# Output projection: eight of 32 row blocks of six chunks in seven products of 2x2 blocks instead of eight

## Chip, cores and metric

The kernel runs on one core of a Trainium2 chip. The metric is the device time of one execution in microseconds (us). The time before is the median of three runs. Engines are named as in the profile: PE is TensorE's matrix multiply and PEld its weight load, DVE is VectorE, ACT is ScalarE, POOL is GpSimd, SP is SyncE, which here only issues transfers (DMAs).

## What is computed

One encoder block on 256 tokens of width 4096, all in float32. Attention and Fourier mixing each give a branch; the branches are gated and merged, projected once more, added to the input and normalised:

```python
def reference(x, norm_gain, w_in, gate_bias, w_branch_attn, w_branch_fourier, w_out, final_norm_gain):
    ...
        h = rms_norm(x, norm_gain[layer])
        proj = h @ w_in[layer]
        ...
        branch_attn = (o_attn * jax.nn.silu(z_attn)) @ w_branch_attn[layer]
        ...
        branch_four = (y_four * jax.nn.silu(z_four)) @ w_branch_fourier[layer]
        ...
        mixed = jax.nn.sigmoid(g_attn) * branch_attn + jax.nn.sigmoid(g_four) * branch_four
        x = x + mixed @ w_out[layer]
    return rms_norm(x, final_norm_gain)
```

The change is in the last two lines: `mixed @ w_out` is a product of 256x4096 by 4096x4096.

## The kernel before

**Matrix products.** The 256 tokens are two halves of 128 (`t` = 0, 1). The weights of a product are read in chunks of 512 columns (`CW`) and, within a chunk, in row blocks of 128 (`k`); `w_out` has 8 chunks of 32 row blocks. Each float32 operand is split into a high half, rounded to the PE's format (`F32R`), and a low half, the rest. A product of two blocks is three matmuls into the same accumulator: high by high, high by low, low by high. The tokens' halves `m_hi` and `m_lo` are kept in SBUF; the weights are split as they come. Each matmul has a 128x128 block of tokens as the loaded operand and 128x512 of weights as the moving one.

**One chunk** is one call of `gemm` (line 236). Its `load` issues a DMA of four row blocks (1 MB) into one of three buffers `wt`, then takes a pair of row blocks at a time: ACT writes the high half (`wh`, 128x1024) and DVE subtracts it from the weights to make the low half (`wl`). `run(i)` issues the split of step i+1, then pending small tasks (`step`), then the twelve matmuls of step i (two row blocks, two halves of tokens, three matmuls). So a chunk is 16 steps.

**Buffers.** `turn` hands out the `wh` and `wl` buffers in rotation: three of each, and more when `spare` lists free tiles (line 231). A buffer is written again only when PE has finished the step that used it, so the number of buffers limits how far ACT and DVE can be ahead of PE. In the output projection there are three sets up to chunk 5 and seven from chunk 6 on.

**Tasks.** Other DVE and ACT work is put in between the splits: a task is a generator that yields the cost of its next piece and a delay in steps, and `step` runs pieces while a budget of 1.45 us a step lasts. `add` (line 881) adds a finished chunk to the residual `x` (in `res`), takes the sum of squares on ACT, and multiplies by the gain `fg`; it begins four steps after the chunk's end. All engines work strictly in the order in which the program issues their instructions.

**The end.** Chunk 7 runs with `LAG` 5: the second half of the tokens goes five steps behind the first, so that the first half's normalisation and stores lie beside matmuls. `last` (line 897) adds, normalises and stores a half.

Of the kernel before, what the change touches and what calls it, by code (L numbers as in the profile page):

```python
# [10 lines left out]
F32 = mybir.dt.float32  # L11
F32R = mybir.dt.float32r
AF = mybir.ActivationFunctionType
ALU = mybir.AluOpType
# [3 lines left out]
P = 128  # L18
D = 4096
SEQ = 256  # L20
NT = SEQ // P
KT = D // P
CW = 512
# [9 lines left out]
WG = 4  # L33
WS = 2
LAG = 5
# [2 lines left out]
BUDGET_U = 0.75  # L38
CAP = 2.7
LEAD = 3  # L40

Q0, K0, V0, ZA0, U0, ZF0, G0 = 0, 3072, 6144, 9216, 10240, 12288, 14336

# [50 lines left out]
def hybrid_block(ctx: ExitStack, tc: tile.TileContext, x, norm_gain, w_in, gate_bias, w_attn,  # L94
                 w_four, w_out, final_gain, rope, mask, dft, out):
    nc = tc.nc
    x = x[0]
    w_in, w_attn, w_four, w_out = w_in[0], w_attn[0], w_four[0], w_out[0]
    pe, dve, act, sp = (InOrder(tc, e) for e in (nc.tensor, nc.vector, nc.scalar, nc.sync))
# [16 lines left out]
    def lower(i, shape, dtype, name):  # L116

        return low.tile(shape, dtype, tag=f"low{i}", name=name)
# [17 lines left out]
    def spawn(task, urgent=True, after=()):  # L136

        t = Task(task, urgent, clock.now + (2 if pending else 0), after)
        if urgent:
            tasks.insert(sum(u.urgent for u in tasks), t)  # L140
        else:
            tasks.append(t)
        return t
# [6 lines left out]
    def finish(these):  # L150
        flush()
        complete(these)

    def complete(these):
        for t in list(these):
            complete(t.after)
            while t in tasks:
                if not t.run(clock.now):
                    tasks.remove(t)
# [17 lines left out]
    def rows(a, t, s):  # L177

        return a.rearrange("(m q) d -> q m d", q=2)[t, :, s]
# [47 lines left out]
    def turn(name, shape, dtype):  # L227
        n = turns[name] = turns.get(name, -1) + 1
        if name == "wt":
            return wtp.tile(shape, dtype, name=f"wt{n % 3}")  # L230
        n %= 3 + len(spare)
        if n < 3:
            return wpool.tile(shape, dtype, name=f"{name}{n}")
        return lower(2 * spare[n - 3] + (name == "wl"), shape, dtype, f"{name}{n}")

    def gemm(accs, hi, lo, w, c0, lag=0, during=None, loading=None, at=None, between=None):

        nk = w.shape[0] // P  # L240
        wv = w[:, c0:c0 + CW].rearrange("(k p) n -> p k n", p=P)
        wt = None
        steps = []

        def load(k):
            nonlocal wt
            if k >= nk:
                return
            single = loading is not None and k == 0
            if k % WG == 0:  # L250
                wt = turn("wt", [P, WG, CW], F32)
                pieces = [(0, WG)] if not single else [(0, 1), (1, 2), (2, WG)]
                for a, b in pieces:
                    sp.dma_start(wt[:, a:b, :], wv[:, k + a:k + b, :])
                    if loading is not None:
                        loading(k + b)
            wh = turn("wh", [P, WS, CW], F32R)
            wl = turn("wl", [P, WS, CW], F32R)
            for j in range(0, WS, 1 if single else WS):
                n = slice(j, j + (1 if single else WS))  # L260
                split(wt[:, k % WG + n.start:k % WG + n.stop, :], wh[:, n], wl[:, n])
            steps.append((wh, wl))

        def multiply(i, j, t):
            if not 0 <= i < len(steps):
                return
            wh, wl = steps[i]
            k = i * WS + j
            a, b = hi[:, k, t * P:(t + 1) * P], lo[:, k, t * P:(t + 1) * P]
            pe.matmul(accs[t], a, wh[:, j, :], start=(k == 0), stop=False)  # L270
            pe.matmul(accs[t], a, wl[:, j, :], start=False, stop=False)
            pe.matmul(accs[t], b, wh[:, j, :], start=False, stop=(k == nk - 1))

        def run(i):
            load((i + 1) * WS)
            if during is not None:
                during(i * WS)
            if at is not None and i == at[0]:
                at[1]()
            step()  # L280
            for j in range(WS):
                for t in range(NT):
                    multiply(i - lag * t, j, t)
                if between is not None and j == 0:
                    between(i * WS)

        load(0)
        flush()
        if during is not None:
            during(-WS)  # L290
        last = nk // WS + lag - 1
        for i in range(last):
            run(i)
        pending.append(lambda: run(last))
# [3 lines left out]
    def new_accs():  # L298
        n = turns["acc"] = turns.get("acc", -1) + 1
        complete(users[n % 2])  # L300
        return [ps_mm.tile([P, CW], F32, name=f"acc{n % 2}{t}") for t in range(NT)]

    def use(task, after=()):

        users[turns["acc"] % 2] = [spawn(task, after=after)]
        return users[turns["acc"] % 2]
# [376 lines left out]
    def mixed():  # L683
        nonlocal sz
        finish(mixing)
        fo.close()
        sz = pool(ctx, "szp").tile([P, NT, 2 * CW], F32, name="sz")
        users[1 - slot] = [spawn(silu_za(0))]
# [185 lines left out]
    with ExitStack() as st:  # L874
        op = pool(st, "op")
        RW = 2 * CW
        res = [[op.tile([P, RW], F32, name=f"res{t}{i}") for i in range(D // RW)] for t in range(NT)]
        parts = op.tile([P, NT, 8], F32, name="fparts")
        fgs = [op.tile([P, CW], F32, name=f"fg{c % 2}") for c in range(8)]

        def add(c, accs):
            s = slice(c * CW, (c + 1) * CW)
            sp.dma_start(fgs[c], final_gain[None, s].to_broadcast([P, CW]))
            if c % 2 == 0:
                for t in range(NT):
                    sp.dma_start(res[t][c // 2], rows(x, t, slice(c * CW, c * CW + RW)))
            yield 0.0, 0
            for t in range(NT):
                rt = res[t][c // 2][:, c % 2 * CW:(c % 2 + 1) * CW]
                yield 0.75, 4 if t == 0 else 0  # L890
                dve.tensor_add(rt, rt, accs[t])
                junk = op.tile([P, CW], F32, name="junk2")
                act.activation(junk, rt, AF.Square, accum_out=parts[:, t, c:c + 1])
                yield 0.6, 0
                dve.tensor_mul(rt, rt, fgs[c])

        def last(accs, t):
            rt = res[t][3][:, CW:]
            yield 0.7, 0
            dve.tensor_add(rt, rt, accs[t])  # L900
            junk = op.tile([P, CW], F32, name="junk2")
            act.activation(junk, rt, AF.Square, accum_out=parts[:, t, 7:8])
            yield 1.0, 0
            ssq = small.tile([P, 1], F32, name="ssq")
            dve.tensor_add(ssq, parts[:, t, 7:8], sums[t])
            r = small.tile([P, 1], F32, name="rstd_o")
            rstd_of(r, ssq)
            for n, (c0, c1) in enumerate(((0, 256), (256, 1024), (1024, 2048), (2048, 3072), (3072, 3584), (3584, 4096))):
                o = res[t][c0 // RW][:, c0 % RW:(c1 - 1) % RW + 1]
                if c0 == 7 * CW:  # L910
                    dve.scalar_tensor_tensor(o, o, r, fgs[7], op0=ALU.mult, op1=ALU.mult)
                elif n % 2:
                    act.activation(o, o, AF.Copy, scale=r)
                else:
                    dve.tensor_scalar(o, o, r, None, op0=ALU.mult)
                sp.dma_start(rows(out[0], t, slice(c0, c1)), o)

        sums = [op.tile([P, 1], F32, name=f"sum{t}") for t in range(NT)]

        def summed():  # L920
            yield 0.2, 2
            for t in range(NT):
                dve.reduce_sum(sums[t], parts[:, t, 0:7], axis=AX.X)

        use(add(0, first))
        for c in range(1, 7):
            accs = new_accs()
            if c == 6:
                spare.extend(range(4))
            gemm(accs, m_hi, m_lo, w_out, c * CW)  # L930
            added = use(add(c, accs))
        spawn(summed(), after=added)
        accs = new_accs()
        sp.dma_start(fgs[7], final_gain[None, 7 * CW:].to_broadcast([P, CW]))
        gemm(accs, m_hi, m_lo, w_out, 7 * CW, LAG, at=(KT // WS, lambda: finish([spawn(last(accs, 0))])))
        finish(list(tasks))
        finish([spawn(last(accs, 1))])

# [50 lines left out]
```

## Time and profile before

| | |
|---|---|
| Median of 3 runs | 2536.12 us (2535.91 to 2537.52) |
| Profiled execution | 2535.88 us |
| Its span | 2534.1 us |
| Granted PE clock, mean over the span | 0.998 |
| Bytes moved by DMA | 529.60 MB, 209 GB/s on average |

A row of a group of instructions reads: line, engine, operation, output <- inputs, shapes, count, then total busy time and mean duration in ns of one, then the idle time ahead of them and what ended it. A row of the timeline reads: start, duration (us), engine, line, operation, and in brackets the idle time ahead and its releaser. A matmul's record lasts longer than its slot, because matmuls overlap in the array.

### The profile page before, as it was taken

To read this page: it belongs to the slowest core of one execution; us is meant where nothing else is said; L and a number is where in the kernel's file an instruction comes from. 1 tells how busy PE (TensorE), PEld (TensorE's weight loads), DVE (VectorE), ACT (ScalarE), POOL (GpSimd) and SP (SyncE) were. 2 spreads that over 40 slices of the span, in tenths; PEclk is the share of its full clock that TensorE was granted. 3 is DMA by queue.
4 is the path that set the end of the run, shared out by engine and by line. 5 is a ranking of instruction groups with operands and counts; after the bars stand their busy time and mean duration, and the time that the engine had idled before them with its cause. 6 is when DMAs were issued, how large, how long until landed. Compare 5 with 4: busy or idle time off the path is not lost.

```text
span 2534.1 us, 29976 instructions
## 1 busy us (share of the span) xinstructions
PE 2518.7 (99%) x11646; PEld 2102.9 (83%) x11646; DVE 1768.8 (70%) x2546; ACT 1121.3 (44%) x1340; POOL 77.7 (3%) x146
## 2 busy tenths in 40 slices
PE   9999999999999999999999999999999999999998
PEld 7888888888888888888888888888888888888886
DVE  6778887777753575848689584878656888754554
ACT  5544544454443434343443434344544444444443
POOL 0000000000000000000000000000100000000000
PEclk9999999999999999999999999999999999999999
DMA  7677666666655565555555555555766665656674
GB/s 256 239 251 233 233 234 227 236 232 217 221 177 172 190 196 187 198 195 188 187 175 190 193 198 189 194 187 179 253 232 216 225 230 188 218 189 223 218 245 150
DMA packets 252846, 529.60 MB, mean 209 GB/s; under 512 B 9984, under 2 KB 10784, under 8 KB 252704
## 3 DMA queue, kind: packets, MB, share of 16 engines
q1 hardware_dynamic: 237056, 471.89, 56.2%
q0 software_dynamic: 15600, 55.78, 6.5%
q8 instruction: 91, 1.49, 0.3%
q14 instruction: 51, 0.42, 0.0%
q10 hardware_dynamic: 48, 0.02, 0.0%
HBM read 512.97 MB, written 14.68 MB: 208 GB/s over the span
## 4 chain that ended last, share of the span: by engine, by line
PE 97%; DMA 1%; DVE 1%; issue 0%; ACT 0%; SPq 0%; DVEq 0%; ACTq 0%
PE acc L53 91%; PE pt L53 3%; PE sc L53 3%; DMA xt<-in_x_dram 1%; DMA wt<-in_w_in_dram 1%; DVE wl L53 0%; ACT wh L53 0%; SPq L53 0%; DVE f_lo L53 0%; DVE res L53 0%; DVE f L53 0%; DVE e L53 0%; ACT xs L53 0%; ACT junk L53 0%; DVEq L985 0%
## 5 line engine op out<-in xcount | busy, mean ns | idle before, releaser
L53 DVE TENSOR_TENSOR wl<-wt,wh 128x1024 fp32r<-128x1024 f32 (+1 forms) x865 | 1056.7, 1224 | 687.2 <-ACT wh L53 679.1
L53 ACT ACTIVATE wh<-wt 128x1024 fp32r<-128x1024 f32 (+1 forms) x865 | 913.5, 1059 | 1266.8 <-PE acc L53 1204.2
L53 PE MATMUL acc<-wh,h_hi 128*128 128x512 f32 x2560 | 1002.1, 391 | 0.0
L53 PE MATMUL acc<-wl,h_hi 128*128 128x512 f32 x2560 | 996.8, 389 | 0.9 <-DVE wl L53 0.8
L53 PE MATMUL acc<-wh,h_lo 128*128 128x512 f32 x2560 | 997.4, 390 | 0.0
L53 PEld LDWEIGHTS acc<-wh,h_lo 128*128 128x128 f32 x2560 | 480.5, 188 | 100.9 <-DVE h_lo L53 0.2
L53 PEld LDWEIGHTS acc<-wl,h_hi 128*128 128x128 f32 x2560 | 480.8, 188 | 98.5 <-DVE wl L53 2.4
L53 PEld LDWEIGHTS acc<-wh,h_hi 128*128 128x128 f32 x2560 | 480.7, 188 | 96.2 <-ACT wh L53 0.3
L53 PE MATMUL acc<-wl,m_hi 128*128 128x512 f32 x512 | 199.2, 389 | 0.0
L53 PE MATMUL acc<-wh,m_lo 128*128 128x512 f32 x512 | 199.2, 389 | 0.0
L53 PE MATMUL acc<-wh,m_hi 128*128 128x512 f32 x512 | 199.2, 389 | 0.0
L53 PEld LDWEIGHTS acc<-wl,m_hi 128*128 128x128 f32 x512 | 96.1, 188 | 20.5 <-DVE wl L53 0.3
L53 PEld LDWEIGHTS acc<-wh,m_hi 128*128 128x128 f32 x512 | 96.1, 188 | 20.1
L53 PEld LDWEIGHTS acc<-wh,m_lo 128*128 128x128 f32 x512 | 96.1, 188 | 19.7
L53 PE MATMUL acc<-wh,y_hi 128*128 128x512 f32 x256 | 99.6, 389 | 0.0
L53 PE MATMUL acc<-wl,y_hi 128*128 128x512 f32 x256 | 99.6, 389 | 0.0
L53 PE MATMUL acc<-wh,y_lo 128*128 128x512 f32 x256 | 99.6, 389 | 0.0
L53 DVE STREAM_TRANSPOSE mT<-m 32x128 f32<-32x128 f32 x256 | 77.4, 302 | 4.0
L53 DVE STREAM_TRANSPOSE pT<-e 32x128 f32<-32x128 f32 x256 | 77.2, 302 | 3.8
L53 DVE STREAM_TRANSPOSE k<-m 32x128 f32<-32x128 f32 x192 | 58.0, 302 | 3.0
L53 DVE STREAM_TRANSPOSE q<-m 32x128 f32<-32x128 f32 x192 | 58.0, 302 | 3.0
L53 PEld LDWEIGHTS acc<-wh,y_hi 128*128 128x128 f32 x256 | 48.1, 188 | 10.1
(154 smaller groups left out, 1643.8 us busy)
## 6 DMA issues: line engine op xcount, KB each, us to landing
wt<-in_w_in_dram SPq DMA_DIRECT2D x319, 1024.0 KB, 5.1
wt<-in_w_out_dram SPq DMA_DIRECT2D x64, 1024.0 KB, 5.5
wu<-in_w_in_dram POOLq DMA_DIRECT2D x64, 512.0 KB, 5.2
wt<-in_w_branch_fourier_dram SPq DMA_DIRECT2D x32, 1024.0 KB, 5.4
wt<-in_w_branch_attn_dram SPq DMA_DIRECT2D x16, 1024.0 KB, 5.4
gates_d<-sg POOLq DMA_DIRECT2D x32, 256.0 KB, 4.5
ga<-gates_d POOLq DMA_DIRECT2D x12, 512.0 KB, 5.0
bias<-in_gate_bias_dram SPq DMA_DIRECT2D x16, 256.0 KB, 5.4
```

Of the source, the lines that this page charges most:

```text
L53: return lambda *a, **k: self.tc.keep_in_program_order(f(*a, **k))
```

## The change

Chunks 2 to 7 are taken in three pairs (c, c+1). For the first eight of the 32 row blocks (`KS`), two row blocks by two chunks form a 2x2 block of weights B, and two halves of tokens by the same two row blocks form a 2x2 block of tokens A. The eight products of blocks are replaced by seven (Winograd's form of Strassen's algorithm), which need sums of blocks:

- sums of tokens S1 to S4, made once for each of the four such groups of row blocks (`token_sums`, from `m_hi` + `m_lo`, split again into `s_hi`, `s_lo`);
- sums of weights T1 to T4, made for each group and pair: one DVE instruction of 128x1024 for two of them and two of 128x512 for the others, in the tile `raw`; each is then split like weights.

`seven` issues one such group: one load of two row blocks by 1024 columns, the sums and splits, and 21 matmuls (seven products of three) instead of 24. Three products go into accumulators of the two chunks; the other four (M1, M5, M6, M7) have PSUM tiles of their own for a pair, the four that `ps_s` and `ps_t` hold, and are added to the residual by `shares` (six additions of 128x512, one of 128x1024) after the first chunk of the pair.

The other 24 row blocks of each of these chunks remain as they were: 12 steps. The four groups of a pair are all issued in its first chunk, behind steps 2, 5, 8 and 10 (`MIX`). From chunk 2 on there are five sets of `wh` and `wl` (`spare` 2, 3; the tiles 0 to 3 hold the sums of tokens), and seven in chunk 7. A group takes three sets and a tile `b11`. `add` loses its gain multiplications to a task `gain`, its delay is dropped for chunks after the first, and the loads of `x` move into `residual`.

```diff
+KS = 8
+MIX = {2: 0, 5: 1, 8: 2, 10: 3}
...
+    def thrice(acc, a, b, wh, wl, start, stop):
+
+        pe.matmul(acc, a, wh, start=start, stop=False)
+        pe.matmul(acc, a, wl, start=False, stop=False)
+        pe.matmul(acc, b, wh, start=False, stop=stop)
...
+            a, b = (v[:, k0 + k, t * P:(t + 1) * P] for v in (hi, lo))
+            thrice(accs[t], a, b, wh[:, j, :], wl[:, j, :], k == 0 and not begun[t], k == nk - 1)
...
+            if mixed is not None:
+                mixed(i)
...
+        def add(c, accs):
             for t in range(NT):
+                yield 0.75, 0 if t or c else 4
+                rt = part(t, c)
                 dve.tensor_add(rt, rt, accs[t])
                 junk = op.tile([P, CW], F32, name="junk2")
                 act.activation(junk, rt, AF.Square, accum_out=parts[:, t, c:c + 1])
+
+        def gain(c):
+            sp.dma_start(fgs[c], final_gain[None, c * CW:(c + 1) * CW].to_broadcast([P, CW]))
+            for t in range(NT):
+                yield 0.7, 0 if t else 4
+                rt = part(t, c)
                 dve.tensor_mul(rt, rt, fgs[c])
...
+        def token_sums(c):
...
+            dve.tensor_add(r, m_hi.tiles[c].bitcast(F32), m_lo.tiles[c].bitcast(F32))
...
+            act.activation(s_hi[c], so, AF.Copy)
+            yield 1.25, 1
+            dve.tensor_tensor(s_lo[c], so, s_hi[c].bitcast(F32), op=ALU.subtract)
+
+        def seven(g, c, first, second, shared):
...
+            def pair(src, between=None):
+                wh = turn("wh", [P, WS, CW], F32R)
+                wl = turn("wl", [P, WS, CW], F32R)
+                act.activation(wh, src, AF.Copy)
+                if between is not None:
+                    between()
+                dve.tensor_tensor(wl, src, wh.bitcast(F32), op=ALU.subtract)
+                return [(wh[:, j, :], wl[:, j, :]) for j in range(WS)]
+
+            def further():
+                dve.tensor_tensor(more[:, 0], wt[:, 3], sums[:, 0], op=ALU.subtract)
+                dve.tensor_tensor(more[:, 1], wt[:, 2], more[:, 0], op=ALU.subtract)
+
+            m1, m5, m6, m7 = shared
+
+            dve.tensor_tensor(sums, wt.rearrange("p (k b) n -> p k b n", k=2)[:, :, 1], wt[:, 0:2], op=ALU.subtract)
+            b21, b22 = pair(wt[:, 2:4])
+            t1, t3 = pair(sums, further)
+            thrice(first[0], *a(1, 0), *b21, False, False)
+            thrice(second[0], *s(3), *b22, begin, False)
+            t2, t4 = pair(more)
+            thrice(m5, *s(0), *t1, begin, end)
+            thrice(m7, *s(2), *t3, begin, end)
+            bh, bl = lower(8, [P, 2, CW], F32R, "b11").rearrange("p (i n) c -> i p n c", i=2)
+            bh, bl = bh[:, 0], bl[:, 0]
+            act.activation(bh, wt[:, 0], AF.Copy)
+            dve.tensor_tensor(bl, wt[:, 0], bh.bitcast(F32), op=ALU.subtract)
+            thrice(m6, *s(1), *t2, begin, end)
+            thrice(first[1], *a(1, 1), *t4, False, False)
+            thrice(m1, *a(0, 0), bh, bl, begin, end)
...
+        spare.extend((2, 3))
+        common = []
+        for c in range(2, 8, 2):
...
+            gemm(accs, m_hi, m_lo, w_out, c * CW, k0=KS, mixed=mixed, at=(3, lambda: residual(c)))
+            common = [spawn(shares(c, shared))]
+            six = added(c, accs, common, slot)
+            if c < 6:
+                gemm(other, m_hi, m_lo, w_out, (c + 1) * CW, k0=KS, begun=(True, False))
+                added(c + 1, other, common)
```

What the new order looks like on the engines is shown at two places of chunk 4. The first is DVE's order late in the chunk. Names carry the buffer's number (`wl3` is the low half in set 3); `wt` is a load, `raw` the sums of weights. Before, steps 11 to 15 of chunk 4 read:

```order
L53 TENSOR_TENSOR wl1_18103<-wt0_18084,wh1_18102 128x1024
L53 TENSOR_TENSOR wl2_18121<-wt1_18118,wh2_18120 128x1024
L53 TENSOR_TENSOR wl0_18137<-wt1_18118,wh0_18136 128x1024
L53 TENSOR_TENSOR wl1_18155<-wt2_18152,wh1_18154 128x1024
L53 TENSOR_TENSOR wl2_18171<-wt2_18152,wh2_18170 128x1024
```

Now the last two of the twelve steps and the fourth group:

```order
L55 TENSOR_TENSOR wl3_18286<-wt0_18283,wh3_18285 128x1024
L55 TENSOR_TENSOR wl4_18302<-wt0_18283,wh4_18301 128x1024
L55 TENSOR_TENSOR raw_18319<-wt1_18317 128x1024
L55 TENSOR_TENSOR wl0_18322<-wt1_18317,wh0_18321 128x1024
L55 TENSOR_TENSOR raw_18319<-wt1_18317,raw_18319 128x512 x2
L55 TENSOR_TENSOR wl1_18326<-raw_18319,wh1_18325 128x1024
L55 TENSOR_TENSOR wl2_18338<-raw_18319,wh2_18337 128x1024
L55 TENSOR_TENSOR b11_18347<-wt1_18317,b11_18347 128x512
```

Where one split followed the other, seven more instructions now stand behind the last step's; that step is written into set 4, and the group takes sets 0, 1 and 2 and `b11`.

The second place is PE's order at the end of the third group, where `b11` is the last product's weights and `acc00` the accumulator of chunk 4:

```order
L55 MATMUL acc01_17970<-wl2_18262,m_hi_14685 128x512
L55 MATMUL acc01_17970<-wh2_18261,m_lo_14693 128x512
L55 MATMUL sc_18047<-b11_18271,m_hi_14685 128x512 x2
L55 MATMUL sc_18047<-b11_18271,m_lo_14693 128x512
L55 MATMUL acc00_17969<-wh4_18225,m_hi_14690 128x512
L55 MATMUL acc00_17969<-wl4_18226,m_hi_14690 128x512
L55 MATMUL acc00_17969<-wh4_18225,m_lo_14698 128x512
```

Before, where step 13 ends and step 14 begins, a step's matmuls follow the last one's with nothing between them:

```order
L53 MATMUL acc00_17904<-wh0_18136,m_lo_14698 128x512
L53 MATMUL acc01_17905<-wh0_18136,m_hi_14690 128x512
L53 MATMUL acc01_17905<-wl0_18137,m_hi_14690 128x512
L53 MATMUL acc01_17905<-wh0_18136,m_lo_14698 128x512
L53 MATMUL acc00_17904<-wh1_18154,m_hi_14691 128x512
L53 MATMUL acc00_17904<-wl1_18155,m_hi_14691 128x512
L53 MATMUL acc00_17904<-wh1_18154,m_lo_14699 128x512
```

Step 9 of the twelve (set 4), whose split stands ahead of the third group on DVE, is multiplied behind it on PE, so set 4 comes free only after the group and the step.

More of the change, by code (lines that the diff above doesn't have):

```diff
@@ L234, in turn, with gemm @@
         return lower(2 * spare[n - 3] + (name == "wl"), shape, dtype, f"{name}{n}")
-    def gemm(accs, hi, lo, w, c0, lag=0, during=None, loading=None, at=None, between=None):
-        nk = w.shape[0] // P
-        wv = w[:, c0:c0 + CW].rearrange("(k p) n -> p k n", p=P)
+    def thrice(acc, a, b, wh, wl, start, stop):
+        pe.matmul(acc, a, wh, start=start, stop=False)
+        pe.matmul(acc, a, wl, start=False, stop=False)
+        pe.matmul(acc, b, wh, start=False, stop=stop)
+    def gemm(accs, hi, lo, w, c0, lag=0, during=None, loading=None, at=None, between=None,
+             k0=0, begun=(False, False), mixed=None):
+        nk = w.shape[0] // P - k0
+        wv = w[k0 * P:, c0:c0 + CW].rearrange("(k p) n -> p k n", p=P)
         wt = None
@@ L268, in multiply @@
             k = i * WS + j
[L269 to L272, printed above, removed]
+            a, b = (v[:, k0 + k, t * P:(t + 1) * P] for v in (hi, lo))
+            thrice(accs[t], a, b, wh[:, j, :], wl[:, j, :], k == 0 and not begun[t], k == nk - 1)
         def run(i):
@@ L879, in hybrid_block, with residual, part @@
         fgs = [op.tile([P, CW], F32, name=f"fg{c % 2}") for c in range(8)]
-        def add(c, accs):
[L882 to L887, printed above, removed]
+        def residual(c):
+            for t in range(NT):
+                sp.dma_start(res[t][c // 2], rows(x, t, slice(c * CW, c * CW + RW)))
+        def part(t, c):
+            return res[t][c // 2][:, c % 2 * CW:(c % 2 + 1) * CW]
+        def add(c, accs):
             for t in range(NT):
-                rt = res[t][c // 2][:, c % 2 * CW:(c % 2 + 1) * CW]
-                yield 0.75, 4 if t == 0 else 0
+                yield 0.75, 0 if t or c else 4
+                rt = part(t, c)
                 dve.tensor_add(rt, rt, accs[t])
@@ L893, in add, with added @@
                 act.activation(junk, rt, AF.Square, accum_out=parts[:, t, c:c + 1])
-                yield 0.6, 0
-                dve.tensor_mul(rt, rt, fgs[c])
+        def gain(c):
+            sp.dma_start(fgs[c], final_gain[None, c * CW:(c + 1) * CW].to_broadcast([P, CW]))
+            for t in range(NT):
+                yield 0.7, 0 if t else 4
+                rt = part(t, c)
+                dve.tensor_mul(rt, rt, fgs[c])
+        def added(c, accs, after=(), slot=None):
+            slot = turns["acc"] % 2 if slot is None else slot
+            users[slot] = [spawn(add(c, accs), after=after)]
+            spawn(gain(c), after=users[slot])
+            return users[slot]
@@ new lines, in hybrid_block @@
+        s_hi, s_lo = ([lower(2 * c + i, [P, 2, 4, P], F32R, v) for c in range(KS // 4)] for i, v in enumerate(("s_hi", "s_lo")))
+        def token_sums(c):
+            yield 1.25, 0
+            raw = op.tile([P, WG, CW], F32, name="raw")
+            r = raw[:, 0:2].rearrange("p a (b n) -> p (a b) n", b=2)
+            dve.tensor_add(r, m_hi.tiles[c].bitcast(F32), m_lo.tiles[c].bitcast(F32))
+            v = raw[:, 0:2].rearrange("p g (j t n) -> p g j t n", j=2, t=2)
+            so = raw[:, 2:4].rearrange("p g (i n) -> p g i n", i=4)
+            for i, x0, x1, op_ in ((0, v[:, :, 0, 1], v[:, :, 1, 1], ALU.add), (1, so[:, :, 0], v[:, :, 0, 0], ALU.subtract),
+                                   (2, v[:, :, 0, 0], v[:, :, 0, 1], ALU.subtract), (3, v[:, :, 1, 0], so[:, :, 1], ALU.subtract)):
+                yield 0.45, 0
+                dve.tensor_tensor(so[:, :, i], x0, x1, op=op_)
+            yield 0.0, 0
+            act.activation(s_hi[c], so, AF.Copy)
+            yield 1.25, 1
+            dve.tensor_tensor(s_lo[c], so, s_hi[c].bitcast(F32), op=ALU.subtract)
@@ new lines, in seven, with a, s @@
+        def seven(g, c, first, second, shared):
+            begin, end = g == 0, g == KS // 2 - 1
+            wt = turn("wt", [P, WG, CW], F32)
+            sp.dma_start(wt.rearrange("p (k b) n -> p k (b n)", k=2),
+                         w_out[2 * g * P:(2 * g + 2) * P, c * CW:(c + 2) * CW].rearrange("(k p) n -> p k n", p=P))
+            raw = op.tile([P, WG, CW], F32, name="raw")
+            sums, more = raw[:, 0:2], raw[:, 2:4]
+            def a(i, t):
+                return [v[:, 2 * g + i, t * P:(t + 1) * P] for v in (m_hi, m_lo)]
+            def s(i):
+                return [v[g // 2][:, g % 2, i, :] for v in (s_hi, s_lo)]
+            def pair(src, between=None):
[25 more added lines that the diff above has]
+            thrice(m1, *a(0, 0), bh, bl, begin, end)
@@ new lines, in shares @@
+        def shares(c, shared):
+            m1, m5, m6, m7 = shared
+            yield 0.75, 1
+            u = gp.tile([P, CW], F32, name="sg", bufs=2)
+            act.activation(u, m1, AF.Copy)
+            dve.tensor_add(part(0, c), part(0, c), m1)
+            yield 0.75, 1
+            dve.tensor_add(u, u, m6)
+            yield 0.75, 0
+            dve.tensor_add(part(0, c + 1), part(0, c + 1), u)
+            yield 0.75, 0
+            dve.tensor_add(u, u, m7)
+            yield 1.3, 0
+            both = res[1][c // 2].rearrange("p (b n) -> p b n", b=2)
+            dve.tensor_add(both, both, u.rearrange("p (b n) -> p b n", b=1).to_broadcast([P, 2, CW]))
+            for t in range(NT):
+                yield 0.75, 0
+                dve.tensor_add(part(t, c + 1), part(t, c + 1), m5)
@@ L923, in summed, with mixed @@
                 dve.reduce_sum(sums[t], parts[:, t, 0:7], axis=AX.X)
-        use(add(0, first))
-        for c in range(1, 7):
-            accs = new_accs()
[L928 to L933, printed above, removed]
+        residual(0)
+        added(0, first)
+        ready = [spawn(token_sums(c), False) for c in range(KS // 4)]
+        accs = new_accs()
+        gemm(accs, m_hi, m_lo, w_out, CW)
+        added(1, accs)
+        spare.extend((2, 3))
+        common = []
+        for c in range(2, 8, 2):
+            accs = new_accs()
+            slot, other, shared = turns["acc"] % 2, [], []
+            def mixed(i):
+                if i not in MIX:
+                    return
+                if not other:
+                    complete(ready + common)
+                    other.extend(new_accs())
+                    shared.extend(p.tile([P, CW], F32, name=n) for p, n in ((ps_s, "sc"), (ps_t, "pt")) * 2)
+                seven(MIX[i], c, accs, other, shared)
+            gemm(accs, m_hi, m_lo, w_out, c * CW, k0=KS, mixed=mixed, at=(3, lambda: residual(c)))
[4 more added lines that the diff above has]
+                added(c + 1, other, common)
+        spawn(summed(), after=six)
+        spare.extend((0, 1))
+        accs = other
         sp.dma_start(fgs[7], final_gain[None, 7 * CW:].to_broadcast([P, CW]))
-        gemm(accs, m_hi, m_lo, w_out, 7 * CW, LAG, at=(KT // WS, lambda: finish([spawn(last(accs, 0))])))
+        gemm(accs, m_hi, m_lo, w_out, 7 * CW, LAG, k0=KS, begun=(True, False),
+             at=((KT - KS) // WS, lambda: finish(common + [spawn(last(accs, 0))])))
         finish(list(tasks))
```

## The prediction

> **What bounds the kernel now.** The first view is the page: busy time by engine, and the chain that ended last.
>
> ```profile
> PE 2518.7 (99%) x11646; PEld 2102.9 (83%) x11646; DVE 1768.8 (70%) x2546; ACT 1121.3 (44%) x1340; POOL 77.7 (3%) x146
> PE 97%; DMA 1%; DVE 1%; issue 0%; ACT 0%; SPq 0%; DVEq 0%; ACTq 0%
> ```
>
> The matrix engine PE never rests, and 97% of the chain is its own work. The second view is that chain in order of time (start, length, what); the third is busy time in the stretch that holds nearly the whole output projection.
>
> ```profile
> 1868.30 654.25 PE acc L53 x2880
> 2200.00:2522.55 322.55, 322.53 (x1423) 266.36 (x1421) 164.33 (x159) 134.75 (x150) 0.00 (x0) 1.00 0.62 205
> ```
>
> From 1868 us to the last matmul there is one unbroken run: 654.25 / 2880 = 0.2272 us a matmul. Here every matmul removed is worth 0.227 us, and every microsecond for which PE waits costs one. VectorE (DVE, third column) works 164 us of 323 and ScalarE (ACT, fourth) 135, so on average they have room. How far they run ahead is in the timelines of ACT, DVE and PE:
>
> ```profile
> 2299.46 1.06 ACT L53 ACTIVATE wh<-wt 128x1024 fp32r<-128x1024 f32 x1 [1.66 <-PE acc L53]
> 2302.18 1.06 ACT L53 ACTIVATE wh<-wt 128x1024 fp32r<-128x1024 f32 x1 [1.66 <-PE acc L53]
> 2300.55 1.23 DVE L53 TENSOR_TENSOR wl<-wt,wh 128x1024 fp32r<-128x1024 f32 x1 [1.49 <-ACT wh L53]
> 2303.27 1.23 DVE L53 TENSOR_TENSOR wl<-wt,wh 128x1024 fp32r<-128x1024 f32 x1 [1.49 <-ACT wh L53]
> ```
>
> Every 2.72 us (twelve matmuls, one step) PE gives a `wh` buffer back, only then ACT writes the next high half, and only then DVE the low half. Their lead is the number of buffers and nothing else, although both idle over half the time.
>
> **What the change removes.** The counted instructions show 36 matmuls fewer: twelve groups, 21 matmuls in place of 24. That is 36 x 0.2272 = **8.2 us** off PE. The last additions and stores after PE's end are the same.
>
> **What it adds.** Durations are these groups' means (third number):
>
> ```profile
> L53 DVE TENSOR_TENSOR wl<-wt,wh 128x1024 fp32r<-128x1024 f32 x143 | 173.7, 1225 | 148.5 <-ACT wh L53 147.5
> L53 ACT ACTIVATE wh<-wt 128x1024 fp32r<-128x1024 f32 x142 | 148.7, 1058 | 196.8 <-PE acc L53 179.0 <-DMA wt<-in_w_out_dram 13.7 <-DVE wl L53 2.9
> L53 DVE TENSOR_TENSOR res<-res,acc 128x512 f32<-128x512 f32 x16 | 10.9, 682 | 4.0 <-PE acc L53 4.0
> L53 ACT ACTIVATE junk<-res 128x512 f32<-128x512 f32 x16 | 10.1, 632 | 30.7 <-DVE res L53 25.1 <-issue 5.6
> L53 DVE TENSOR_TENSOR res<-res,fg 128x512 f32<-128x512 f32 x14 | 9.7, 693 | 11.4 <-ACT junk L53 11.4
> L53 ACT ACTIVATION_READ_ACCUMULATOR junk<-res 128x1 f32 x16 | 3.0, 186 | 0.0
> L53 DVE TENSOR_TENSOR m<-ga 128x512 f32<-128x512 f32 x4 | 2.6, 685 | 0.0
> ```
>
> A group costs DVE four instructions of 128x1024 and three of 128x512: 4 x 1.225 + 3 x 0.685 = 6.96 us, beside 21 x 0.2272 = 4.77 us of PE. The 128x1024 differences of weights with a plain f32 result are in no row; I give them the 1.225 of the split. On average it fits: the first half of a pair, with its additions and gains, has 12 x 1.225 + 4 x 6.96 + 2 x 0.682 + 2 x 0.693 = 45.3 us of DVE beside 12 x 2.726 + 4 x 4.77 = 51.8 of PE. But a group is more DVE work than PE work, so it must be done ahead, and the five buffer sets don't let it. Steps are called S0 to S11 and groups G0 to G3; PE runs G0 after S2, G1 after S5, G2 after S8, G3 after S10; in DVE's order the step behind each group on PE (S3, S6, S9, S11) stands ahead of it. A group takes three sets, so S5 needs the set of S3, S8 that of S6, S11 that of S9, and PE runs each of those three just behind a group. DVE stands still during the group and then must do everything for the next one.
>
> From PE's end of S3, S6 or S9 the clock runs so: 0.2 us until ACT starts (a matmul record of 0.389 outlasts its 0.227 slot by 0.16, and an engine wakes 0.03 after its releaser in the timeline above), 1.06 of ACT, 0.04, then DVE at 1.225 each, and 0.04 to PE. PE meets the first low half at a group's second matmul.
>
> - **G1**: DVE has S5, the two gains of the chunk before (2 x 0.69), S6, the differences and the first low half: 0.2 + 1.06 + 0.04 + 4 x 1.225 + 1.38 + 0.04 = 7.62. PE has two steps and one matmul, 5.68. It waits 1.94.
> - **G2**: the same without gains: 6.24 against 5.68, a wait of 0.56.
> - **G3**: one step nearer: S11, differences, low half: 5.02 against 2.95, a wait of 2.06.
> - **G0**: the two additions of the last chunk now stand ahead of S2 and wait for that chunk's last matmul. Additions to 1.56, ACT's second square (0.632 + 0.186) to 2.42, S2's high half to 3.48; then DVE does S2, S3, differences and low half, 8.42 with the wakings. PE needs it at 3 x 2.726 + 0.227 = 8.41. Nothing to speak of.
> - In every group the next low half comes two 128x512 and one 128x1024 later, 1.37 + 1.225 + 0.04 = 2.64, while PE has six matmuls, 1.36: a **second wait** of 1.28. The third low half (1.225 later) and the last (0.685) are in time, for PE has six matmuls before each.
>
> Per pair: 1.3 + 3.22 + 1.84 + 3.34 = 9.7; three pairs 29.1. A stopped PE also starts late:
>
> ```profile
> 28.16 1.23 DVE L53 TENSOR_TENSOR wl<-wt,wh 128x1024 fp32r<-128x1024 f32 x1 [2.62 <-ACT wh L53]
> 29.44 0.50 PE L53 MATMUL acc<-wl,h_hi 128*128 128x512 f32 x1 [0.76 <-DVE wl L53]
> 29.78 0.40 PE L53 MATMUL acc<-wh,h_lo 128*128 128x512 f32 x1
> ```
>
> Here PE waits for a low half, goes on 0.05 us after DVE, and its next matmul comes after 0.34 us, not 0.227: 0.11 lost. The restart after a first wait only shortens the second, so it counts once a group: 12 x 0.11 = 1.3.
>
> **The last chunk** starts with five steps of six matmuls (1.36 us), and DVE has the seven new additions of `shares` among them. Counted from G3's end: S0 needs the set of G3's third pair and its low half is done at 1.85; S1 3.07, S2 4.3, an addition 4.98, S3 6.2, three additions 8.26, S4 9.5. PE wants S4's at 2.73 + 4 x 1.363 + 0.23 = 8.41: a wait of 1.1. The broadcast addition and S5 bring another 1.1, then DVE is level. With restarts 2.4. In the second halves of the other pairs steps are 2.73 long, and the same count leaves over 2 us in hand.
>
> Three edits cost nothing. The sums of tokens, at most 2 x (2 x 1.225 + 4 x 0.69) = 10.4 us of DVE (the four short ones at the price of twice their length), lie in chunk 1, where DVE has half of 43.6 us free; uncovered they would cost that. The residual loads move on SP's queue by some steps, long before their use. Weight bytes are equal, and a group's load is issued early:
>
> ```profile
> wt<-in_w_out_dram SPq DMA_DIRECT2D x64, 1024.0 KB, 5.5
> DMA to landing us min/median/max: 5.3/5.5/12.6
> ```
>
> G2 has least: its load waits for S7's low half, just before G1's end, and DVE wants it 2.73 + 0.2 + 1.06 + 2 x 1.225 = 6.4 us later; 5.5 fits.
>
> **Sum.** 29.1 + 1.3 + 2.4 - 8.2 = +24.6. The profiled execution took 2535.88 us (a span of 2534.1 and 1.8 around it, 0.2 under the median), so **2560.5 us**. For the differences of weights I bound from below by this spacing,
>
> ```profile
> 2316.76 0.69 DVE L53 TENSOR_TENSOR res<-res,fg 128x512 f32<-128x512 f32 x1 [0.79 <-ACT junk L53]
> 2317.37 0.68 DVE L53 TENSOR_TENSOR res<-res,acc 128x512 f32<-128x512 f32 x1
> ```
>
> where one instruction starts 0.08 before the other ends. If all seven in a group's chain did, the sum would fall by 12 x 7 x 0.08 = 6.7, to 2554; as much above the rows gives 2567. I take the middle.
>
> **The rivals.**
> - *The cover holds (faster).* PE never waits, and the time is 2535.9 - 8.2 = 2527.7. For it: DVE's average load, 45.3 of 51.8. Against it: the rows of ACT waiting for PE. It decides at a wait of 0.68 us a group (8.2 / 12); below that the change gains. DVE would have to hold a whole group ready ahead, which takes three sets more. Chance 0.10.
> - *Half the waits.* If the chain is shorter than I count (high halves released sooner, instructions overlapping), waits of 0.7 to 1.6 us a group give 2536 to 2547. Chance 0.17, of which 0.05 within 0.2%.
> - *A late load.* If a group's load takes the 12.6 us maximum instead of 5.5, G2 waits 6 us longer: 3 x 6 = 18, 2578. Against: the median. Chance 0.08.
> - *The clock.* These rows are windows around the end of PE's work (behind the five engines comes the granted clock):
>
> ```profile
> 2522.00:2526.00 4.00, 0.53 (x3) 0.10 (x1) 2.15 (x9) 1.37 (x4) 0.00 (x0) 1.00 0.92 363
> 2526.00:2530.00 4.00, 0.00 (x0) 0.00 (x0) 1.62 (x3) 1.53 (x2) 0.00 (x0) 0.55 0.77 302
> 2530.00:2534.00 4.00, 0.00 (x0) 0.00 (x0) 0.00 (x0) 0.00 (x0) 0.00 (x0) 0.50 0.56 222
> ```
>
> PE's long run ends at 1868.3 + 654.25 = 2522.55, and 0.55 over the second window means that the clock fell at 2526.4, nearly 4 us later; my longest wait is 2 us. If it fell in every group, 21 matmuls at half speed would cost 4.8 us more, 12 x 4.8 = 57, 2618. Chance 0.02. The Trainium skill, "TensorE: Matmul & The Clock Gate" (Part 1: The HAM clock gate), has the clock halve after a whole idle window of about 3.4 us; by it, too, waits of 2 us with work between them leave the clock alone, and the rows agree.
>
> **How the numbers follow.** Forecast 0.63, with its own range of 2547 to 2572. To hold 8 in 10 I take in most of the half-waits case below: 2541 to 2572; the loads, the clock, the full cover and a little of the half waits stay out. A measurement tells about 0.2% (5 us) from no change. Faster 0.10, within 0.2% 0.05, slower 0.85.
>
> **What would show it.** PE's count falls by 36. In the profile after, PE has idle time with DVE `wl` as releaser, some 30 us in all, in chunks 2, 4, 6 and at the start of 7; two waits in most groups, the largest first ones in G3 and G1; ACT's high half of S5, S8 and S11 released by PE just behind a group. DVE busy time rises by about 80 us (12 x (6.96 - 2 x 1.225) + 3 x (6 x 0.685 + 1.225) and the sums of tokens). I am wrong if PE's run stays unbroken, if DMA `wt` is the releaser, or if the granted clock drops below 1.00 before the end.

## The result, and the profile after

| | before | changed |
|---|---|---|
| Median | 2536.55 us (4 runs) | 2556.91 us (4 runs, 2556.52 to 2557.6) |
| Ratio | | 1.0079, 95% interval 1.0067 to 1.0091 |
| Span of the profiled execution | 2534.1 us | 2555.8 us |

The changed kernel is 20.4 us slower; 2560.5 was forecast. The ratios of the experiments go by runs of the kernel before that were taken along with them (medians 2536.79 and 2536.92). The page of the changed kernel, busy time and the chain that ended last:

```profile
PE 2521.1 (99%) x11610; PEld 2097.0 (82%) x11610; DVE 1836.2 (72%) x2639; ACT 1139.4 (45%) x1369; POOL 77.6 (3%) x146
PE 93%; DVE 4%; issue 1%; ACT 1%; DMA 1%; SPq 0%; DVEq 0%; ACTq 0%
```

PE has 36 matmuls fewer and still 99%, a share that hides the matter: 99% of a span that is 22 us longer. The chain shows it: PE's part falls from 97% to 93%, and DVE has 4% of it instead of 1%. In order of time (start, length, what), the chain in chunk 4 now reads:

```profile
2369.89 2.74 PE acc L55 x12
2374.94 1.29 DVE res L55 x2
2380.96 1.15 DVE wl L55
2383.61 4.86 issue
2390.71 1.22 DVE wl L55
2395.53 1.15 DVE wl L55
2396.72 1.42 PE pt L55 x5
2400.20 2.73 PE acc L55 x12
2405.25 1.22 DVE raw L55
2408.93 1.15 DVE wl L55
2410.12 1.43 PE pt L55 x5
```

One unbroken run of 2880 matmuls has become a chain that changes between PE and DVE at every group. The timeline of PE shows what each change costs (in brackets the idle time and its releaser); these are groups 1, 2 and 3 of chunk 4, two rows each:

```profile
2379.69 0.50 PE L55 MATMUL acc<-wl,m_hi 128*128 128x512 f32 x1 [1.41 <-DVE wl L55]
2382.15 0.50 PE L55 MATMUL pt<-wl,s_hi 128*128 128x512 f32 x1 [0.81 <-DVE wl L55]
2394.25 0.50 PE L55 MATMUL acc<-wl,m_hi 128*128 128x512 f32 x1 [0.20 <-DVE wl L55]
2396.72 0.50 PE L55 MATMUL pt<-wl,s_hi 128*128 128x512 f32 x1 [0.81 <-DVE wl L55]
2407.66 0.50 PE L55 MATMUL acc<-wl,m_hi 128*128 128x512 f32 x1 [1.80 <-DVE wl L55]
2410.12 0.51 PE L55 MATMUL pt<-wl,s_hi 128*128 128x512 f32 x1 [0.80 <-DVE wl L55]
```

Each of these three groups waits twice for a low half, the first waits are largest in groups 3 and 1, and group 0 has none. And the timelines of ACT and DVE around group 1 show why:

```profile
2366.79 1.05 ACT L55 ACTIVATE wh<-wt 128x1024 fp32r<-128x1024 f32 x1
2372.70 2.96 ACT L55 ACTIVATE wh<-wt 128x1024 fp32r<-128x1024 f32 x3 [4.87 <-PE acc L55]
2368.15 1.22 DVE L55 TENSOR_TENSOR wl<-wt,wh 128x1024 fp32r<-128x1024 f32 x1
2373.80 1.23 DVE L55 TENSOR_TENSOR wl<-wt,wh 128x1024 fp32r<-128x1024 f32 x1 [4.43 <-ACT wh L55]
2374.94 1.29 DVE L55 TENSOR_TENSOR res<-res,fg 128x512 f32<-128x512 f32 x2
2376.14 1.22 DVE L55 TENSOR_TENSOR wl<-wt,wh 128x1024 fp32r<-128x1024 f32 x1
2377.28 1.22 DVE L55 TENSOR_TENSOR raw<-wt 128x1024 f32<-128x1024 f32 x1
2378.41 1.22 DVE L55 TENSOR_TENSOR wl<-wt,wh 128x1024 fp32r<-128x1024 f32 x1
2379.55 1.42 DVE L55 TENSOR_TENSOR raw<-wt,raw 128x512 f32<-128x512 f32 x2
2380.88 2.52 DVE L55 TENSOR_TENSOR wl<-raw,wh 128x1024 fp32r<-128x1024 f32 x2
```

After step 4's split DVE idles 4.43 us, for ACT waits 4.87 us for PE to give a set back. Then DVE works without a gap, step 5, two gains, step 6, differences, first low half, and PE waits for the end of that row (2378.41 + 1.22 = 2379.63; PE goes on at 2379.69).

**The account.** From the projection's first matmul on `m_hi` to the last matmul it is 348.0 us before and 368.5 after, 20.5 more; with the 8.2 removed, 28.7 us were lost. A wait costs the idle time of its row, 0.16 more because a matmul's record outlasts its slot by that (0.389 against 0.227), and 0.11 at the start after it. Counted from start to start against a slot of 0.2267, chunk 4's four groups lose 0.3, 2.9, 1.6 and 3.2 us, 7.9 in all, chunk 6's 8.0 and chunk 2's 8.5, 24.4 for the three pairs. Chunk 1 loses 1.3 and the last chunk 3.0, at these waits:

```profile
2235.99 0.50 PE L55 MATMUL acc<-wl,m_hi 128*128 128x512 f32 x1 [0.42 <-DVE wl L55]
2241.97 0.51 PE L55 MATMUL acc<-wl,m_hi 128*128 128x512 f32 x1 [0.24 <-DVE wl L55]
2514.83 0.50 PE L55 MATMUL acc<-wl,m_hi 128*128 128x512 f32 x1 [0.53 <-DVE wl L55]
2517.10 0.50 PE L55 MATMUL acc<-wl,m_hi 128*128 128x512 f32 x1 [0.61 <-DVE wl L55]
2523.75 0.50 PE L55 MATMUL acc<-wl,m_hi 128*128 128x512 f32 x1 [0.76 <-DVE wl L55]
```

These make up the 28.7. What chunk 2 lost more than the others, 0.6, comes from a fall of the clock in its last group (last section). The profiled execution's other 1.2 us lie ahead of the projection, where nothing was changed.

### The profile page after: what moved, and what is told of

Read it like the earlier page. It is cut to its first block, busy times and chain, and to the rows that moved or that the text cites. A ratio compares the mean times of both kernels' runs of the same rounds, so it can differ in the third digit from the quotient of the medians.

```text
span 2555.8 us, 30034 instructions
## 1 busy us (share of the span) xinstructions
PE 2521.1 (99%) x11610; PEld 2097.0 (82%) x11610; DVE 1836.2 (72%) x2639; ACT 1139.4 (45%) x1369; POOL 77.6 (3%) x146
## 4 chain that ended last, share of the span: by engine, by line
PE 93%; DVE 4%; issue 1%; ACT 1%; DMA 1%; SPq 0%; DVEq 0%; ACTq 0%
PE acc L55 85%; PE pt L55 4%; PE sc L55 3%; DVE wl L55 2%; DVE raw L55 1%; ACT wh L55 1%; DMA wt<-in_w_in_dram 1%; DVE res L55 0%; ACT junk L55 0%; DVE e L55 0%; DVE f L55 0%; SPq L55 0%; DVE f_lo L55 0%; DVE sg L55 0%; DVE s_lo L55 0%
## 5 line engine op out<-in xcount | busy, mean ns | idle before, releaser
L55 DVE TENSOR_TENSOR wl<-wt,wh 128x1024 fp32r<-128x1024 f32 (+1 forms) x853 | 1041.5, 1223 | 637.8 <-ACT wh L55 630.2
L55 ACT ACTIVATE wh<-wt 128x1024 fp32r<-128x1024 f32 (+1 forms) x853 | 898.1, 1059 | 1211.3 <-PE acc L55 1139.6
L55 PE MATMUL acc<-wl,m_hi 128*128 128x512 f32 x440 | 172.9, 393 | 12.8 <-DVE wl L55 12.8
L55 PE MATMUL acc<-wh,m_lo 128*128 128x512 f32 x440 | 171.7, 390 | 0.0
L55 PE MATMUL acc<-wh,m_hi 128*128 128x512 f32 x440 | 171.5, 390 | 0.0
L55 PEld LDWEIGHTS acc<-wl,m_hi 128*128 128x128 f32 x440 | 82.6, 188 | 35.4 <-DVE wl L55 18.6
L55 PEld LDWEIGHTS acc<-wh,m_hi 128*128 128x128 f32 x440 | 82.6, 188 | 17.4 <-ACT wh L55 0.3
L55 PEld LDWEIGHTS acc<-wh,m_lo 128*128 128x128 f32 x440 | 82.7, 188 | 16.7
L55 PEld LDWEIGHTS acc<-wh,y_lo 128*128 128x128 f32 x256 | 48.1, 188 | 10.0
```

Of the source, the lines that this page charges most:

```text
L55: return lambda *a, **k: self.tc.keep_in_program_order(f(*a, **k))
```

## Experiments

The theory: PE waits because DVE gets its buffer sets back only behind a group, and then needs longer for the next group than PE for the steps ahead of it. The main rival: DVE simply has too much to do in these half chunks. Diffs are against the changed kernel unless another is named.

**Seven products without the sums of weights.** The group uses the four plain blocks, split in two pairs.

```diff
-            dve.tensor_tensor(sums, wt.rearrange("p (k b) n -> p k b n", k=2)[:, :, 1], wt[:, 0:2], op=ALU.subtract)
             b21, b22 = pair(wt[:, 2:4])
-            t1, t3 = pair(sums, further)
+            b11, b12 = pair(wt[:, 0:2])
...
-            t2, t4 = pair(more)
-            thrice(m5, *s(0), *t1, begin, end)
+            thrice(m5, *s(0), *b12, begin, end)
```

> The sums of weights are left out: the seven products of each group use the four plain weight blocks, split as before (two splits a group instead of four and a half). The output is not the reference's. The 36 matmuls are still gone, and the sums of tokens, the shares and the accumulators are as in the changed kernel. Theory: a group then takes two sets, step 5 needs step 2's set and no wait is left in the groups; what stays is the removal of 8.2 us, against some 3 us of waits at the start of the last chunk and 1.2 us in chunk 1: about 2532.5. Rival (seven products in separate accumulators cost PE more each than the eight did, or the shares cost something): 2537 or more.

Measured: 2530.77 us, ratio to before 0.9975 (0.9965 to 0.9985). PE waits in chunk 1 and at the last chunk's start only, none in the groups. The kernel is 6.0 us faster than before, and the waits that are left cost 2.0: the removal is worth the 8.2 that it was priced at, and apart from these waits the shares, the sums of tokens and the separate accumulators don't eat it up. This run takes away DVE's work and a buffer set at once, so it doesn't tell theory and rival apart; the next two do.

**The same work, PE's order changed.** PE multiplies a group behind the next step, whose set is so given back before the group; the group itself is needed a step later, too. The last chunk's rotation starts at another set.

```diff
         def run(i):
...
+            while held:
+                held.pop()()
             if mixed is not None:
-                mixed(i)
+                held.extend(mixed(i))
...
-            thrice(first[0], *a(1, 0), *b21, False, False)
...
+            def multiplied():
+                thrice(first[0], *a(1, 0), *b21, False, end)
...
+            return multiplied
...
         spare.extend((0, 1))
         accs = other
+        for v in ("wh", "wl"):
+            turns[v] += (3 - turns[v]) % 7
```

> The same work, but PE runs each group's 21 matmuls behind the next step instead of ahead of it, so that the set which the next but one split waits for comes free before the group and not behind it (and the last chunk's rotation starts at a set that is free then). Theory: DVE gets a step and the whole group's time more, 5 and more us, the waits of about 1 to 2 us in groups 1, 2 and 3 all vanish; 2536.5 - 8.2 removed, + 1.2 in chunk 1, + about 2.7 at the start of the last chunk: 2532, between 2530 and 2536. Rival (DVE has too much to do on average): the waits move to the next group, and the time stays above 2545.

Measured: 2532.51 us, ratio 0.9982 (0.9973 to 0.9991). The page's first part, and all waits of PE in the projection (total, times, longest):

```profile
PE 2512.3 (99%) x11610; PEld 2095.7 (83%) x11610; DVE 1837.5 (73%) x2639; ACT 1141.7 (45%) x1369; POOL 77.9 (3%) x146
PE acc L55 <- DVE wl L55: 2.4, 5, 0.8
```

DVE's 2639 instructions and its busy time are the changed kernel's, and the time is 24 us less: PE has no wait in chunks 2 to 6. The rival falls. Five waits are left, those of chunk 1 and of the last chunk.

**The same order, one buffer set more.**

```diff
         if n < 3:
             return wpool.tile(shape, dtype, name=f"{name}{n}")
+        if spare[n - 3] is None:
+            return more_sets[0].tile(shape, dtype, name=f"{name}{n}")
...
-                junk = op.tile([P, CW], F32, name="junk2")
+                junk = op.tile([P, CW], mybir.dt.bfloat16, name="junk2")
...
-        spare.extend((2, 3))
+        spare.extend((2, 3, None))
+        more_sets.append(op)
```

> The changed kernel's order and work, with a sixth buffer set from chunk 2 on (and eight in the last chunk; the unused result of the squares is stored in half the width to make room). Step 5 then waits for step 2's set instead of step 3's, step 11 for step 8's: all come free ahead of a group. Theory (sets, not work): the first waits of groups 1 and 3 go, and most of the others; about 20 us less than the changed kernel, 2534 to 2541. Rival (DVE has too much to do): 2555 or more. My own first count said that three sets more were needed; by it one more would leave half of the waits, 2545.

Measured: 2541.2 us, ratio 1.0016 (1.0007 to 1.0026), 15.7 us under the changed kernel and just past the expected end. PE's waits in chunks 2 to 6, by releaser (total, times, longest), first of the changed kernel, then with six sets:

```profile
PE acc L55 <- DVE wl L55: 10.2, 9, 1.8
PE pt L55 <- DVE wl L55: 6.5, 8, 0.8
```

```profile
PE pt L55 <- DVE wl L55: 2.8, 9, 0.6
```

All first waits (on `acc`) are gone, and the second ones (on `pt`) more than halved. So the number of sets is enough to move it, with the order and DVE's work (2639 instructions) as they were; only ACT writes the unused squares in half the width. In the last chunk, which has eight sets here, the first wait grew from 0.53 to 1.53 us, so the chunks 2 to 6 gained more than the time shows. Still, the kernel is not faster than before: one set more takes most of the loss away, not all.

**The gains one step earlier**, into the time in which DVE idles.

```diff
         def gain(c):
...
-                yield 0.7, 0 if t else 4
+                yield 0.7, 0 if t else 3
```

> The gain multiplications of the chunk before are released one step earlier, so that they stand ahead of step 5's split on DVE, where DVE idles for 4.4 us in the changed kernel, and not behind it. Same work in all. Theory (a chain that starts when a buffer set comes free): the first wait of group 1 falls from 1.41 us to about 0.2, as in group 2, 1.2 us in each of three pairs: 3.6 us less than the changed kernel, about 2553. Rival (DVE has too much to do on average in that half chunk): the same work, so no change, 2557.

Measured: 2554.76 us, ratio 1.0071 (1.0056 to 1.0086), 2.2 under the changed kernel. The waits of chunks 2 to 6:

```profile
PE acc L55 <- DVE wl L55: 6.6, 9, 1.8
PE pt L55 <- DVE wl L55: 6.0, 8, 0.8
```

10.2 has become 6.6, the 3.6 us expected: group 1's first wait is now 0.21. Not all of it reaches the time: the projection is 2.9 us shorter in this profile, for the clock fell in two groups instead of one (last section), and the two medians' intervals overlap. The waits agree with the theory, the gain in time alone would not settle it.

**The edits around the groups alone**, all row blocks in plain products.

```diff
-        ready = [spawn(token_sums(c), False) for c in range(KS // 4)]
...
-            gemm(accs, m_hi, m_lo, w_out, c * CW, k0=KS, mixed=mixed, at=(3, lambda: residual(c)))
-            common = [spawn(shares(c, shared))]
-            six = added(c, accs, common, slot)
+            gemm(accs, m_hi, m_lo, w_out, c * CW, at=(3, lambda: residual(c)))
+            six = added(c, accs)
```

> Only the edits around the groups: add and gain as two tasks, the delay dropped, the residual loads moved, five buffer sets from chunk 2 and seven in chunk 7, all 32 row blocks in plain products. Theory: these edits cost nothing, 2536 to 2537. Rival (the moved additions or loads hold DVE or the queue up): 2540 or more, with waits of PE.

Measured: 2542.94 us, ratio 1.0022 (1.0013 to 1.0031). My expectation was wrong by 6 us, and the time is the one that the rival gave, though not for its reason, as the next run shows. All of PE's waits lie at the start of the last chunk (0.77, 1.63 and 0.76 us), and behind the last of them the clock fell to half for 3.4 us, some 1.7 us more. The timeline of ACT shows the cause:

```profile
2476.98 1.06 ACT L55 ACTIVATE wh<-wt 128x1024 fp32r<-128x1024 f32 x1 [9.82 <-PE acc L55]
2479.70 1.06 ACT L55 ACTIVATE wh<-wt 128x1024 fp32r<-128x1024 f32 x1 [1.66 <-PE acc L55]
```

The rotation changes from five sets to seven there, its next place is a set that was used two steps ago, and ACT waits 9.8 us for it while free sets lie unused. Then five steps of 1.36 us follow, with no lead.

**The same with seven sets from chunk 6 on** (against the last kernel).

```diff
             accs = new_accs()
+            if c == 6:
+                spare.extend((0, 1))
             gemm(accs, m_hi, m_lo, w_out, c * CW, at=(3, lambda: residual(c)))
...
-        spare.extend((0, 1))
         accs = other
```

> The tasks-alone kernel (2542.9), but with seven buffer sets from chunk 6 on, as before the change, instead of from chunk 7. Theory (its 6 us lie at the start of the last chunk, where the rotation of seven starts with sets still in use, so that the five steps ahead are not there): 2536.5 to 2537.5. Rival (the additions, which now wait for PE ahead of a split, cost it): 2541 to 2543.

Measured: 2537.64 us, ratio 1.0004 (0.9995 to 1.0013): no change from before that can be told. The place at which the rotation grows cost the 5.3 us between the two kernels. One wait of PE is left, 0.77 us early in the last chunk, at a split behind ACT's two squares of chunk 6's additions; with its restart it costs 1.1, and the moved additions, gains and loads cost no more than that.

**The best version.** The deferred groups, five sets already in chunk 1, and later shares in the last pair (against the deferred kernel).

```diff
+        spare.extend((2, 3))
         gemm(accs, m_hi, m_lo, w_out, CW)
         added(1, accs)
-        spare.extend((2, 3))
...
-            yield 0.75, 1
+            yield 0.75, 1 if c < 6 else 4
...
-                yield 0.7, 0 if t else 4
+                yield 0.7, 0 if t or c == 6 else 4
...
-             at=((KT - KS) // WS, lambda: finish(common + [spawn(last(accs, 0))])))
+             at=((KT - KS) // WS, lambda: finish(list(tasks) + [spawn(last(accs, 0))])))
```

> The deferred groups (2532.5), and two more edits: five buffer sets already in chunk 1, so that the sums of tokens have more lead, and in the last pair the shares three steps later and the gain at once, so that they lie in steps of twelve matmuls and not of six. Theory: the two waits in chunk 1 (1.2 us) go, and most of the three at the start of the last chunk (2.7 us): 2529, between 2528 and 2531. Rival (the last chunk's waits come from the rotation that grows there, not from the shares): 2531 to 2532.

Measured: 2530.03 us, ratio 0.9973 (0.9963 to 0.9983), faster than both kernels. One wait of PE is left in the whole projection (0.77 us in the last chunk); and the chain that ended last, in order of time (start, length, what), has runs of PE such as this one of 1782 matmuls, without another engine in between:

```profile
1870.08 405.25 PE acc L55 x1782
```

Of the 8.2 us that the change removes, 6.9 are now in the time.

## Why the prediction was right, and where it was off

- **8.2 us removed**: right. With the sums left out (6.0 in the time and 2.0 in the waits left) and with the deferred order (4.3 and 3.9) they appear.
- **DVE stands still behind a group, and the next group comes late**: right in mechanism and place. It rests on two runs: the set given back earlier by PE's order (24 us, with the group needed a step later as well), and one set more with both orders as they were (16 us). In both the last chunk's rotation differs too, which changed its waits by no more than some 1 us.
- **The sizes of the waits**: too large, 29.1 + 1.3 against 23.8 (the three pairs without the fall of the clock); by the rows PE idles 19.3 us in all, not some 30. I put a whole duration, 1.225, for each DVE instruction of the chain. The durations are right (the new differences take 1219 ns), but an instruction starts 0.08 us before the one ahead of it ends: 2376.14, 2377.28, 2378.41, 2379.55 above are 1.14 apart. My waits count from the end of a slot, so 0.16 has to be added to the idle time of a row: the first waits of groups 1 to 3 were 1.57, 0.36 and 1.96 instead of 1.94, 0.56 and 2.06, and the second ones 0.97 instead of 1.28. With five, three, two and three overlaps of 0.08 in these chains the differences come out to within 0.1. DVE's busy time shows them as well: it rose by 67.4 us, forecast about 80; the durations add up to 78.0 more, and the page counts an overlap once. This overlap was in a row that I quoted as the lower bound.
- **Group 0**: its second wait, forecast at 1.28, was just covered. Half a microsecond is overlap again. The rest is a wrong wait in my count: I let the additions wait for the last matmul of the chunk before, but the first one needs only its own accumulator, done three matmuls earlier. It starts at 2356.06, while chunk 4's first matmul starts at 2356.54; I had it 0.2 behind that.
- **Some luck**: the 6.6 us by which the waits in the pairs were too large were in part made good by what the sum left out or had too small, 1.3 in chunk 1, 0.6 in the last chunk and 0.6 of the clock. So the total missed by 4 us only.
- **The restart**: I counted 0.11 once a group. The rows have it behind every wait, and twice in group 0, whose low halves come just in time.
- **The last chunk**: 2.4 forecast, 3.0 found. The first two waits are those of the forecast (a sum of 1.14 idle, 1.5 with the 0.16 added, against 2.2); a third, 0.76, was not seen: a split behind ACT's two squares. That the late shares cause the first two is supported by the best version, where shares and gains are moved and these two go; the deferred kernel, with the same rotation in the last chunk, has all three. The third stays there, and in the edits alone with seven sets, which have no shares.
- **Three edits cost nothing**: wrong for the sums of tokens. Their 8 us of DVE lie in a chunk with half of DVE free, but with three sets' lead a burst reaches PE: 1.3 us. With five sets in chunk 1 it is nothing.
- **"which takes three sets more"**, in the faster rival: one more took 16 us away, because it frees the one set that hung behind a group. But 2.8 us of waits stayed in the groups and the kernel did not beat the one before, so how many sets a full cover takes is not shown.
- **The clock**: wrong, at a small price. I left it alone at waits of 2 us, and it fell once, in the middle of the projection; that was one of my signs of being wrong. It cost 0.6 us net. The rival's 57 us did not come.

## What to carry to other kernels

Work moved from the bottleneck to an engine that idles nearly half of the time (DVE was busy for 187.7 of the projection's 348.4 us before) is not hidden by that idle time: count, from the moment a buffer comes free, how long the chain on the helping engines takes and how long the bottleneck runs meanwhile. Where the work comes in bursts, the order in which the bottleneck gives buffers back decides; here exchanging two neighbours in PE's order turned 20 us of loss into 4 us of gain. And when a rotation of buffers grows, look at which buffer its next place is.

## What the runs showed of the hardware that was not expected

The clock can fall after a wait much shorter than the 3.8 us after which it fell at the end of the kernel before. In the changed kernel, group 3 of chunk 2 (PE's busy time first, the granted clock behind the engines):

```profile
2313.00:2314.00 1.00, 0.00 (x0) 0.00 (x0) 1.00 (x2) 0.30 (x1) 0.00 (x0) 1.00 0.52 86
2314.00:2315.00 1.00, 0.21 (x1) 0.21 (x2) 1.00 (x2) 0.75 (x1) 0.00 (x0) 1.00 0.86 162
2315.00:2316.00 1.00, 1.00 (x4) 0.77 (x4) 0.96 (x3) 0.00 (x0) 0.00 (x0) 0.59 0.98 371
2316.00:2317.00 1.00, 1.00 (x4) 0.59 (x2) 1.00 (x2) 0.84 (x1) 0.00 (x0) 0.50 0.98 373
2317.00:2318.00 1.00, 1.00 (x3) 0.65 (x3) 0.95 (x2) 1.00 (x3) 0.00 (x0) 0.50 0.19 74
2318.00:2319.00 1.00, 1.00 (x5) 0.81 (x4) 1.00 (x3) 0.69 (x1) 0.00 (x0) 0.70 0.00 0
```

A wait of 1.79 us ends at 2314.79, and the clock falls to half at 2315.2 for some 3.4 us, while PE is already at work: the matmuls come 0.42 apart, and 0.41 + 0.50 + 0.50 + 0.30 = 1.7 us are lost; as the group's second wait did not come, 0.6 of it is left. The same wait in chunks 4 and 6 had no such fall; with the gains moved it came in two groups of three, and in the edits alone it came behind the waits of 1.63 and 0.76. The Trainium skill, "TensorE: Matmul & The Clock Gate" (Part 1: The HAM clock gate), speaks of at least one idle window of about 3.4 us, free-running. The 3.4 us of the fall agree; a fully idle window does not, for PE was idle for 1.8 us only.

The traces narrow down the share. Each of the four falls before a projection's end lasts 3.413 us, and the two falls of the changed kernel, at 2315.18 and at 2547.28 behind its last matmul, lie 68 times 3.413 apart. Cut the output projections of the nine traces, up to the fall behind each, into such windows, so that the falls lie on their borders: PE idled for at least 1.79 us in 13 of them, and each of these ends in a fall; in all others it idled for 1.63 or less (1.63 with six sets), and none does. So between 1.63 and 1.79 us, about half a window, decides here, and a wait of 1.79 us counts whole only if no border cuts it: chunk 4's is cut into 1.47 and 0.32. This is read from the traces, no run tries it, and one fall does not fit: 13.55 us into the best version's execution, behind 1.36 us of idle time.
